# A hybrid decoder step on one core: a sixth weight buffer in one pool, and the operand sets' differences from held rows and from parts summed on GpSimd

## The chip, the cores and the metric

One core of one Trainium2 chip runs the whole kernel. Its engines work side by side, each through its own instructions in order: TensorE (PE, with its weight loads as PEld) multiplies, VectorE (DVE) and ScalarE (ACT) do elementwise work, GpSimd (Pool) does elementwise work beside them, and SyncE (SP) only issues transfers. Transfers between device memory and on-chip memory are issued from the queues of SP, ACT and Pool. The metric is the device time of one execution in microseconds; lower is better.

## The reference, cut to what matters

The reference is one step of a decoder layer for 512 prompt tokens and 64 sample tokens (8 sequences of 8), 576 columns in all, with 2048 features. What counts here are its dense products:

```
u = rmsnorm(x) @ w_in                 # 2048 x 18496: z, x/B/C, dt, q, k, v, gate, mix_s, mix_a
y = ssd(...)                          # 4096 wide, gated and group-normed
o = attention(...) * silu(g_attn)     # 2048 wide
p_ssm  = y @ w_ssm_branch             # 4096 x 2048
p_attn = o @ w_attn_branch            # 2048 x 2048
merged = sigmoid(mix_s) * p_ssm + sigmoid(mix_a) * p_attn
x = x + merged @ w_out                # 2048 x 2048
y_out = rmsnorm(x)
```

All values are fp32. Every operand is split into a rounded high part (fp32r) and a low part, and each product is made of three matmuls: high by high, high by low, low by high.

## The kernel before

Activations lie transposed: feature tiles of 128 rows by 576 columns, as pairs `hk[k]` (high `ah`, low `al`) for k = 0 to 15. A half `j` is 288 of the 576 columns (`TH`). `hb[i][j]` is the quarter of rows 8i to 8i+7 and columns of half j. The weights come in blocks of 1024 x 128 (512 KB), `raw`, and are split into `wh` (ACT, line 80) and `wl` (DVE, line 81).

Two forms of product alternate. In the plain form (`run_main`, matmuls on line 345) one output column of 128 features takes two weight blocks and 2 x 8 x 3 x 2 matmuls of 128 x 288. In the paired form (`pairs_of`, matmuls on line 453) two output columns at a time are made by a seven-product scheme of Strassen's kind: 7 x 8 x 3 matmuls instead of 8 x 8 x 3. For it the weights of a pair, A11, A21, A12 and A22, are loaded (line 380) and combined into S1 to S4 on DVE (`sum_`, line 393). The activations are combined into three further operand sets, the forms: with u1, u2 the two halves of row tile k and v1, v2 those of row tile k + 8,

```
t1 = u2 - u1        t2 = v2 - t1        t3 = v2 - u2        t6 = v1 - t2
```

t2, t3 and t6 live in the tiles `tt` (named t1k, t3k, t6k in the profile); t1 takes the place of the quarter `hb[0][1]` (called `b12`), so it is parked in device memory and brought back when the quarter is free. In a pair, product i = 2 is the first that reads it. `evict` adds up the products (line 404), `merge_out` multiplies by the gate `sg` (line 1345) and writes or accumulates into `mg_d` from Pool's queue (lines 1350 and 1352).

Stages, in order: norm and transposes; six plain columns of mix_a, beside which `sums_job` makes the first forms out of the quarters; 22 pairs for the gates and z (the first paired stage, about 123 to 628 us), beside which `bias_job` writes sixteen blocks of `bias_d` from Pool (line 491); attention; the SSD; two plain columns; then three sets: attention branch, first half of the SSM branch, second half. Each set has a **head** of four plain columns (`FIRST_OUT`) and a **run** of six pairs. Last comes w_out in the plain form.

A set begins with its activations: `acts_in` loads sixteen row tiles of 288 KB (`stg`, line 1309, SP's queue) and splits them (ACT line 1169, DVE line 1170). For the next set this is called during the last pair: rows 0 to 3 after product 2, 4 to 7 after product 3, 8 to 15 after product 6. In the head `forms_job` loads the same rows a second time (lines 1320 to 1322: u1, u2, and the whole v tile), makes t1 and t2 on DVE (1323, 1325), parks t1 from Pool's queue (1324), makes t3 and t6 on Pool (1328, 1329) and splits them all. Near the head's end the run's first weights are loaded and t1 is fetched back into eight `e` tiles.

The pools: `rs` has five tiles of 4 KB a partition, shared by the row tiles, the forms' tiles, A12, A22 and the sums; `raw` in `wp` has two, for A11, A21 and every weight block of the plain form; `ev` (tag `e`) has fourteen of 288 columns, for evictions, gates and fetched t1. A load into a tile waits until its last reader is done. The order of instructions on each engine is set by a scheduler that replays the program with its own model of times; each queue then keeps that order.

Of the kernel before, what the change touches and what calls it, by code (L numbers as in the profile page):

```python
# [34 lines left out]
OFF_XBC = DI  # L35
OFF_DT = OFF_XBC + CONV
# [19 lines left out]
N_E = 14  # L56
# [29 lines left out]
def hybrid(ctx, tc, x_prompt, x_sample, cache_k, cache_v, state_conv, state_ssm, norm_w, w_in, conv_w,  # L86
# [37 lines left out]
    mg_d = scratch([D, T], "mg_d")  # L124
    oh_d = scratch([HEADS * BL], "oh_d")
# [240 lines left out]
    def pairs_of(w, r0, cols, ops, takes, after):  # L366
# [8 lines left out]
        def load(p, *names):  # L375
            for x in names if p < n else ():
                c, kh = cols[p] + P * (x in ("A21", "A22")), x in ("A12", "A22")
                t_ = (rs if kh else wp).tile([P, 8, P], F32, tag="rs" if kh else "raw", name="raw",
                                             bufs=5 if kh else 2)
                sync.dma_start(out=t_, in_=w[r0 + 1024 * kh:r0 + 1024 * kh + 1024, c:c + P].rearrange("(k p) n -> p k n", p=P))  # L380
                st[p][x] = t_

        def sum_(p, x):
            if p >= n:
                return
            s_ = st[p]
# [6 lines left out]
            vec.tensor_tensor(out=s_[x], in0=s_[a], in1=s_[b], op=op)  # L393
# [36 lines left out]
        def run():  # L430
            for p in range(n):
                for i in range(7):
# [729 lines left out]
    b12, t1 = hb[0][1], []  # L1162
# [10 lines left out]
    def sums_job():  # L1173

        yield from wait(36)
        for k in range(8):
# [9 lines left out]
            t1.append(x[0, 0])  # L1186
# [12 lines left out]
    def t1_there():  # L1199

        for k in range(8):
            split_half(b12[k], t1[k])

    def b12_again(p, i):
        if (p, i) == (-len(cols), 0):
            t1_there()
# [12 lines left out]
    drain()  # L1219
    ms.close()  # L1220
# [57 lines left out]
    for g in range(G):  # L1278
        seq.append(m_in(OFF_XBC + (32 + g) * P, take_conv(32 + g)))
        seq.append(m_in(OFF_XBC + (40 + g) * P, take_conv(40 + g)))  # L1280
        for t in range(4):
            seq.append(m_in(OFF_XBC + (4 * g + t) * P, take_conv(4 * g + t) if t < 3 else last_x(g)))
# [20 lines left out]
    def staged_rows():  # L1303
        return rs.tile([P, 8, P], F32, tag="rs", name="stg", bufs=5).rearrange("p a b -> p (a b)")

    def acts_in(src, ks):
        for k in ks:
            t_ = staged_rows()
            sync.dma_start(out=t_[:, :T], in_=src[k * P:(k + 1) * P, :])
            split_half(hk[k], t_[:, :T])  # L1310

    tt = [[tpair(f"t{i}{k}") for k in range(8)] for i in (1, 3, 6)]

    def forms_job(src):

        for k in range(8):
            u, v = staged_rows(), staged_rows()
            u1, t1_, u2, v1, v2, t2_ = (t_[:, i * TH:(i + 1) * TH] for t_, i in ((u, 0), (u, 1), (u, 2), (v, 0), (v, 1),
                                                                            (v, 2)))
# [3 lines left out]
            vec.tensor_tensor(out=t1_, in0=u2, in1=u1, op=ALU.subtract)  # L1323
            pool.dma_start(out=xb_d[k * P:(k + 1) * P, :], in_=t1_)
            vec.tensor_tensor(out=t2_, in0=v2, in1=t1_, op=ALU.subtract)
            yield
            split_half(tt[0][k], t2_)
            pool.tensor_tensor(out=u2, in0=v2, in1=u2, op=ALU.subtract)
            pool.tensor_tensor(out=v1, in0=v1, in1=t2_, op=ALU.subtract)
            yield  # L1330
            split_half(tt[1][k], u2)
# [48 lines left out]
    for i in range(3):  # L1380
# [4 lines left out]
        def last_chunk():  # L1385
            head()
            for k in range(8):
                t1.append(etile("x"))
                sync.dma_start(out=t1[k], in_=xb_d[k * P:(k + 1) * P, :])
# [4 lines left out]
        quick.append(forms_job(src))  # L1394
# [155 lines left out]
```

## Time and profile before

| | us |
|---|---|
| runs shown: median of three (lowest to highest) | 3226.87 (3225.44 to 3229.58) |
| the profiled execution, whole | 3228.93 |
| the profiled execution, span from first to last instruction | 3226.8 |
| plain columns at the start, 24.7 to 122.6 | 97.9 |
| first paired stage, 122.7 to 628.5 | 505.8 |
| heads of the three sets | 56.2, 62.4, 61.5 |
| runs of the three sets | 135.3, 138.7, 140.1 |
| mean granted TensorE clock | 0.983 |

A page of the profile gives the busy time of each engine, the transfers and the costliest groups of instructions; L345 in it is line 345 of the kernel before. A stretch is a window of time in which the busy times are summed again. The waits of an engine name the instruction that waited and the last thing it waited for. A busy TensorE is pipelined, so the number of matmuls in a stretch says more of its pace than its busy time.

### The profile page before, as it was taken

How to read it: one execution, taken by the hardware profiler on the slowest of the kernel's cores; microseconds unless marked ns; L12 is line 12 of the kernel's file. 1: busy time of each engine (PE TensorE's matmuls, PEld its weight loads, DVE VectorE, ACT ScalarE, POOL GpSimd, SP SyncE). 2: the span in 40 equal slices, each digit the busy share in tenths (PEclk: the TensorE clock that was granted, in tenths of full speed). 3: DMA queues.
4: the chain of work that ended last, by engine and by line, in shares of the span. 5: the costliest groups of instructions: out<-in, count | busy, mean ns of one | idle time of the engine just before them, and what ended most of it. 6: DMA issues, size and time to landing. Idle time of an engine off the chain costs nothing. (4 is left out here: it accounts for less than half of the span.)

```text
span 3226.8 us, 58215 instructions
## 1 busy us (share of the span) xinstructions
PE 3112.4 (96%) x22939; PEld 2993.4 (93%) x22939; DVE 1996.5 (62%) x3434; ACT 1473.7 (46%) x2761; POOL 482.5 (15%) x591
## 2 busy tenths in 40 slices
PE   6989999999999999999999999999999999999997
PEld 5989999999898998999999999998899989998997
DVE  6656666515444443477687687686657777877354
ACT  5434444423554554455555555565433433434333
POOL 3200000000001010112213212212221031311111
PEclk9999999999999999999999999999999999999999
DMA  6564444433343243364464564565575676967655
GB/s 198 143 156 121 122 123 125 117 89 90 84 121 93 82 123 100 100 165 135 135 179 128 147 166 132 148 166 146 147 234 175 194 212 143 249 159 194 180 161 158
DMA packets 733650, 471.18 MB, mean 146 GB/s; under 512 B 45433, under 2 KB 696969, under 8 KB 733185
## 3 DMA queue, kind: packets, MB, share of 16 engines
q1 hardware_dynamic: 691616, 420.51, 46.6%
q0 software_dynamic: 24336, 29.20, 4.4%
q10 hardware_dynamic: 17424, 17.76, 1.7%
q8 instruction: 180, 2.95, 0.4%
q14 instruction: 94, 0.76, 0.1%
HBM read 385.79 MB, written 91.81 MB: 148 GB/s over the span
## 5 line engine op out<-in xcount | busy, mean ns | idle before, releaser
L80 ACT ACTIVATE wh<-raw 128x1024 fp32r<-128x1024 f32 x586 | 620.1, 1058 | 1031.6 <-PE ps L453 488.4
L81 DVE TENSOR_TENSOR wl<-raw,wh 128x1024 fp32r<-128x1024 f32 x586 | 728.0, 1243 | 529.9 <-ACT wh L80 525.9
L345 PE MATMUL ps<-ah,wh 128*128 128x288 f32 (+2 forms) x4384 | 1021.4, 302 | 34.8 <-ACT craw L828 10.1
L345 PE MATMUL ps<-ah,wl 128*128 128x288 f32 (+2 forms) x4384 | 1012.6, 301 | 3.5 <-DVE wl L81 3.3
L345 PE MATMUL ps<-al,wh 128*128 128x288 f32 (+2 forms) x4384 | 1012.4, 300 | 2.5 <-DVE al L1170 2.5
L345 PEld LDWEIGHTS ps<-ah,wh 128*128 128x128 f32 x4384 | 735.2, 192 | 50.5 <-issue 11.1
L345 PEld LDWEIGHTS ps<-ah,wl 128*128 128x128 f32 x4384 | 734.5, 191 | 19.6 <-issue 10.6
L345 PEld LDWEIGHTS ps<-al,wh 128*128 128x128 f32 x4384 | 734.6, 191 | 9.0 <-DVE al L1170 4.1
L453 PE MATMUL ps<-ah,wh 128*128 128x288 f32 x1280 | 382.2, 299 | 13.8 <-DVE w L404 5.6
L453 PE MATMUL ps<-ah,wl 128*128 128x288 f32 x1280 | 383.5, 300 | 5.9 <-DVE wl L81 5.4
L453 PE MATMUL ps<-al,wh 128*128 128x288 f32 x1280 | 381.8, 298 | 0.0
L453 PEld LDWEIGHTS ps<-ah,wh 128*128 128x128 f32 x1280 | 244.4, 191 | 14.7 <-issue 5.8
L393 DVE TENSOR_TENSOR raw<-raw 128x1024 f32<-128x1024 f32 x160 | 194.8, 1220 | 97.6 <-DMA raw<-in_w_in_dram 40.6
L453 PEld LDWEIGHTS ps<-ah,wl 128*128 128x128 f32 x1280 | 244.6, 191 | 9.3 <-DVE wl L81 9.2
L453 PEld LDWEIGHTS ps<-al,wh 128*128 128x128 f32 x1280 | 244.7, 191 | 0.1
L844 DVE SCALAR_TENSOR_TENSOR cacc<-craw,prm,cacc 128x600 f32<-128x600 f32 x144 | 126.8, 885 | 45.4 <-ACT cacc L842 43.7
L882 ACT ACTIVATE L<-L,nacs_n 128x128 f32<-128x128 f32 (+1 forms) x320 | 96.7, 379 | 56.6 <-DVE L L879 56.1
L610 DVE CUSTOM_DVE_ANT_0 sc<-bank,bm 128x256 f32<-128x256 f32 (+1 forms) x128 | 43.8, 388 | 80.0 <-PE bank L606 72.1
L923 POOL TENSOR_TENSOR xl<-xe,xh 128x512 fp32r<-128x512 f32 x32 | 58.6, 1832 | 200.3 <-ACT xh L922 199.9
L879 DVE TENSOR_TENSOR L<-L,nacs_n 128x512 f32<-128x512 f32 (+1 forms) x80 | 51.9, 662 | 47.7 <-DMA L<-nacs_d 47.3
L1093 DVE SCALAR_TENSOR_TENSOR s<-s,dec_s,bank 128x128 f32<-128x128 f32 x256 | 70.4, 340 | 10.3 <-PE bank L1087 9.3
L1241 POOL DMA_DIRECT2D dska<-in_d_skip_dram x1 | 0.6, 586 | 455.9 <-DMA z_d<-c 455.9
(575 smaller groups left out, 4497.7 us busy)
## 6 DMA issues: line engine op xcount, KB each, us to landing
raw<-in_w_in_dram SPq DMA_DIRECT2D x306, 512.0 KB
raw<-in_w_ssm_branch_dram SPq DMA_DIRECT2D x64, 512.0 KB
raw<-in_w_out_dram SPq DMA_DIRECT2D x64, 512.0 KB
L<-nacs_d SPq DMA_DIRECT2D x64, 256.0 KB
s<-in_state_ssm_dram SPq DMA_DIRECT2D x64, 256.0 KB
out_dram<-s SPq DMA_DIRECT2D x64, 256.0 KB
raw<-in_w_attn_branch_dram SPq DMA_DIRECT2D x32, 512.0 KB
stg<-y_d SPq DMA_DIRECT2D x48, 288.0 KB
```

Source lines behind the costliest of these rows:

```text
L80: pin(nc.scalar.activation(wh, raw, AF.Copy))
L81: pin(nc.vector.tensor_tensor(out=wl, in0=raw, in1=wh, op=ALU.subtract))
L345: ten.matmul(sums[i][:, s, :part.shape[1]], a[:, kk, :], part, start=(k == 0 and q == 0), stop=(k == last and q == 2))
L393: vec.tensor_tensor(out=s_[x], in0=s_[a], in1=s_[b], op=op)
L453: ten.matmul(st[p]["ps", i][:, :TH], a[:, k, :], b, start=i < 4 and k == 0 and q == 0, stop=k == 7 and q == 2, skip_group_check=i >= 4)
L610: vec.tensor_tensor_reduce(out=s_[:, i, lo:256], in0=ps[:, i, lo:256], in1=bm[j][:, i, lo:256], scale=1.0, scalar=-3e38, op0=ALU.add, op1= ...
L844: vec.scalar_tensor_tensor(out=acc[:, :600], in0=raw[:, i:i + 600], scalar=prm[:, i * 48 + j:i * 48 + j + 1], in1=acc[:, :600], op0=ALU.mu ...
L879: vec.tensor_tensor(out=l_[:rows, :, :n], in0=l_[:rows, :, :n], in1=nacs_n[:rows, blk, h:h + 4].unsqueeze(2).to_broadcast([rows, 4, n]), o ...
L882: act.activation(l_[:rows, i, :n], l_[:rows, i, :n], AF.Exp, scale=-1.0, bias=nacs_n[:rows, blk, h + i:h + i + 1])
L923: pool.tensor_tensor(out=xl, in0=xe, in1=xh, op=ALU.subtract)
L1093: vec.scalar_tensor_tensor(out=sts[i][:, t, :], in0=sts[i][:, t, :], scalar=dec_s[:, 4 * g + t, b:b + 1], in1=ps[:, v, i, :], op0=ALU.mult ...
L1241: pool.dma_start(out=dska, in_=AP(d_skip, 0, [[0, P], [1, H]]))
```

## The change

What the change does:

- The `rs` pool has six tiles instead of five, `ev` eleven instead of fourteen. A21 is loaded into an `rs` tile, so that only A11 is left of a pair in `raw`; the next pair's loads are asked for in the order A21, A22, A11.
- In the first stage t1 goes to a new buffer in device memory, `t1_d`, and is fetched back after the six plain columns; before, it stayed in eight `e` tiles.
- In `acts_in` the sixteen row loads move from SP's queue to Pool's. The tiles of rows 8 to 11 are kept (`staged`, `N_HELD`).
- In `forms_job` u1 and u2 are no longer loaded: one Pool add of high and low part makes both. For k = 0 to 3 v is the kept tile; for k = 4 to 7 it is loaded as before. t3 and t6 are made on DVE instead of Pool.

The renamed offset in the diff (`OFF_XBC`) changes nothing else.

```diff
-N_E = 14
+N_HELD = 4
+N_E = 11
...
+    t1_d = scratch([D // 2, TH], "t1_d")
...
-                t_ = (rs if kh else wp).tile([P, 8, P], F32, tag="rs" if kh else "raw", name="raw",
-                                             bufs=5 if kh else 2)
+                t_ = weights_tile() if x != "A11" else wp.tile([P, 8, P], F32, tag="raw", name="raw", bufs=2)
...
-                s_[x] = rs.tile([P, 8, P], F32, tag="rs", name="raw", bufs=5)
+                s_[x] = weights_tile()
...
-                        load(p + 1, "A11", "A21", "A22")
+                        load(p + 1, "A21", "A22", "A11")
...
+    def weights_tile(name="raw"):
+        return rs.tile([P, 8, P], F32, tag="rs", name=name)
...
-                       for n_, b_ in (("tx", 1), ("rs", 5), ("ev", N_E))))
+                       for n_, b_ in (("tx", 1), ("rs", 6), ("ev", N_E))))
...
-            t1.append(x[0, 0])
+            pool.dma_start(out=t1_d[k * P:(k + 1) * P, :], in_=x[0, 0])
...
     drain()
+    for k in range(8):
+        t1.append(etile("x"))
+        sync.dma_start(out=t1[k], in_=t1_d[k * P:(k + 1) * P, :])
     ms.close()
...
     def acts_in(src, ks):
         for k in ks:
             t_ = staged_rows()
-            sync.dma_start(out=t_[:, :T], in_=src[k * P:(k + 1) * P, :])
+            pool.dma_start(out=t_[:, :T], in_=src[k * P:(k + 1) * P, :])
             split_half(hk[k], t_[:, :T])
+            if 8 <= k < 8 + N_HELD:
+                staged.append(t_)
...
-    def forms_job(src):
+    def forms_job(src, rows):
         for k in range(8):
-            u, v = staged_rows(), staged_rows()
...
-            sync.dma_start(out=u1, in_=src[k * P:(k + 1) * P, :TH])
-            sync.dma_start(out=u2, in_=src[k * P:(k + 1) * P, TH:])
-            sync.dma_start(out=v[:, :T], in_=src[1024 + k * P:1024 + (k + 1) * P, :])
+            u = staged_rows()
+            u1, t1_, u2 = (u[:, i * TH:(i + 1) * TH] for i in range(3))
+            pool.tensor_tensor(out=u[:, :3 * TH].rearrange("p (a b) -> p a b", a=3)[:, 0:3:2, :], in0=sq(hk[k][0]),
+                               in1=sq(hk[k][1]), op=ALU.add)
+            if k < len(rows):
+                v = rows[k]
+            else:
+                v = staged_rows()
+                sync.dma_start(out=v[:, :T], in_=src[1024 + k * P:1024 + (k + 1) * P, :])
+            v1, v2, t2_ = (v[:, i * TH:(i + 1) * TH] for i in range(3))
+            yield
             vec.tensor_tensor(out=t1_, in0=u2, in1=u1, op=ALU.subtract)
-            pool.dma_start(out=xb_d[k * P:(k + 1) * P, :], in_=t1_)
+            pool.dma_start(out=t1_d[k * P:(k + 1) * P, :], in_=t1_)
             vec.tensor_tensor(out=t2_, in0=v2, in1=t1_, op=ALU.subtract)
+            vec.tensor_tensor(out=u2, in0=v2, in1=u2, op=ALU.subtract)
             yield
             split_half(tt[0][k], t2_)
-            pool.tensor_tensor(out=u2, in0=v2, in1=u2, op=ALU.subtract)
-            pool.tensor_tensor(out=v1, in0=v1, in1=t2_, op=ALU.subtract)
+            split_half(tt[1][k], u2)
+            vec.tensor_tensor(out=v1, in0=v1, in1=t2_, op=ALU.subtract)
             yield
-            split_half(tt[1][k], u2)
             split_half(tt[2][k], v1)
             yield
```

The scheduler places the instructions anew. Three places matter for what follows; a row is a line of the kernel (before or after), the operation, what it writes and reads, the shape of a tile, and how often it repeats.

Pool's queue between the first and the second set, before: the last pair's writes of w, o and the two c, then the forms of the second set.

```order
L1352 DMA mg_d<-w 128x288
L1352 DMA mg_d<-o 128x288
L1352 DMA mg_d<-c 128x288 x2
L1324 DMA xb_d<-stg 128x288
L1328 TENSOR_TENSOR stg<-stg 128x288
```

The same place after, with the row loads (line 1315) and the adds (1329):

```order
L1315 DMA stg<-y_d 128x576 x7
L1367 DMA mg_d<-w 128x288
L1315 DMA stg<-y_d 128x576 x3
L1367 DMA mg_d<-o 128x288
L1315 DMA stg<-y_d 128x576 x2
L1367 DMA mg_d<-c 128x288 x2
L1315 DMA stg<-y_d 128x576 x2
L1329 TENSOR_TENSOR stg<-ah_227,al_228 128x2x288
L1329 TENSOR_TENSOR stg<-ah_229,al_230 128x2x288
L1339 DMA t_d<-stg 128x288 x2
```

The row loads have come in among the writes; the last two of them, rows 14 and 15, stand behind both c. Next SP's queue at the end of the second head, before: `raw` on line 73 is the plain form's weight block, on line 380 the first pair's; x is t1 on its way back.

```order
L1320 DMA stg<-y_d 128x288
L1321 DMA stg<-y_d 128x288
L1341 DMA sg<-ms_d 128x288
L1322 DMA stg<-y_d 128x576
L380 DMA raw<-in_w_ssm_branch_dram 128x8x128 x2
L1341 DMA sg<-ms_d 128x288
L380 DMA raw<-in_w_ssm_branch_dram 128x8x128 x2
L1341 DMA sg<-ms_d 128x288
L380 DMA raw<-in_w_ssm_branch_dram 128x8x128
L1389 DMA x<-xb_d 128x288 x8
```

And after:

```order
L1335 DMA stg<-y_d 128x576 x2
L1356 DMA sg<-ms_d 128x288
L382 DMA raw<-in_w_ssm_branch_dram 128x8x128
L1335 DMA stg<-y_d 128x576
L382 DMA raw<-in_w_ssm_branch_dram 128x8x128 x4
L1356 DMA sg<-ms_d 128x288
L1404 DMA x<-t_d 128x288 x8
```

Of the forms' loads only four of 288 KB are left on SP (the last three stand here), and the first pair's weights follow them directly. Last Pool's queue in the first plain columns, before, where `out_dram<-in_cache` are copies of the caches:

```order
L1181 DMA xb_d<-x 128x288
L1251 DMA sinks_s<-sink_d 64x4x1 x2
L529 DMA out_dram<-in_cache_k_dram 2x4x15360 x4
L529 DMA out_dram<-in_cache_v_dram 2x4x15360 x4
L1181 DMA xb_d<-x 128x288 x7
```

And after:

```order
L1186 DMA xb_d<-x 128x288
L1191 DMA t_d<-x 128x288
L1186 DMA xb_d<-x 128x288
L1191 DMA t_d<-x 128x288
L1186 DMA xb_d<-x 128x288 x2
L1191 DMA t_d<-x 128x288 x2
```

The writes of t1 alternate with those of the quarter, and the cache copies are gone from here: they now follow the sixteen bias writes and the load of `dska`.

More of the change, by code (lines that the diff above doesn't have):

```diff
@@ L34 @@
 NEG = -1e30
-OFF_XBC = DI
-OFF_DT = OFF_XBC + CONV
+OFF_xb_dC = DI
+OFF_DT = OFF_xb_dC + CONV
 OFF_Q = OFF_DT + H
@@ L1197, in hybrid @@
     back = []
-    def t1_there():
-        for k in range(8):
-            split_half(b12[k], t1[k])
+    t1 = []
     def b12_again(p, i):
         if (p, i) == (-len(cols), 0):
-            t1_there()
+            for k in range(8):
+                split_half(b12[k], t1[k])
         elif (p, i) == (-1, 1):
@@ L1219, in hybrid @@
     drain()
+    for k in range(8):
+        t1.append(etile("x"))
+        sync.dma_start(out=t1[k], in_=t1_d[k * P:(k + 1) * P, :])
     ms.close()
@@ L1278, in hybrid @@
     for g in range(G):
-        seq.append(m_in(OFF_XBC + (32 + g) * P, take_conv(32 + g)))
-        seq.append(m_in(OFF_XBC + (40 + g) * P, take_conv(40 + g)))
+        seq.append(m_in(OFF_xb_dC + (32 + g) * P, take_conv(32 + g)))
+        seq.append(m_in(OFF_xb_dC + (40 + g) * P, take_conv(40 + g)))
         for t in range(4):
-            seq.append(m_in(OFF_XBC + (4 * g + t) * P, take_conv(4 * g + t) if t < 3 else last_x(g)))
+            seq.append(m_in(OFF_xb_dC + (4 * g + t) * P, take_conv(4 * g + t) if t < 3 else last_x(g)))
         seq += left[:MIXES_S[g]]
@@ L1303, in staged_rows @@
     def staged_rows():
-        return rs.tile([P, 8, P], F32, tag="rs", name="stg", bufs=5).rearrange("p a b -> p (a b)")
+        return weights_tile("stg").rearrange("p a b -> p (a b)")
     def acts_in(src, ks):
@@ L1388, in last_chunk @@
                 t1.append(etile("x"))
-                sync.dma_start(out=t1[k], in_=xb_d[k * P:(k + 1) * P, :])
+                sync.dma_start(out=t1[k], in_=t1_d[k * P:(k + 1) * P, :])
         head, run = pairs_of(w, r0, [n * P for n in range(FIRST_OUT, KT, 2)], ops,
@@ L1393, in hybrid @@
                              on_products((KT - FIRST_OUT) // 2, t1, nxt, sets[i + 1][2], *sets[i + 1][:2], 14 if i == 2 else KT))
-        quick.append(forms_job(src))
+        quick.append(forms_job(src, staged[-N_HELD:]))
         run_main([(w_loads(w, r0, n * P), hx, by_halves(takes[n])) for n in range(FIRST_OUT)], raws=raws, then=last_chunk)
```

5 lines of the change are left out of this document (2 added, 3 removed).

## The prediction

> **What bounds the kernel now.** I read the page first, then a table of stretches, then what each engine waits for in the worst stretches. The page's first rows:
>
> ```profile
> span 3226.8 us, 58215 instructions
> PE 3112.4 (96%) x22939; PEld 2993.4 (93%) x22939; DVE 1996.5 (62%) x3434; ACT 1473.7 (46%) x2761; POOL 482.5 (15%) x591
> ```
>
> TensorE is the bound, so a change can only win where TensorE stands still. The table of stretches shows where that is; its columns are the stretch, its length, then busy time and instruction count of each engine, granted clock, DMA share and GB/s:
>
> ```profile
> 300.00:400.00 100.00, 100.00 (x758) 100.00 (x757) 68.96 (x74) 40.36 (x53) 0.00 (x0) 1.00 0.43 121
> 24.70:122.60 97.90, 91.06 (x643) 86.93 (x641) 76.40 (x172) 47.28 (x104) 19.97 (x27) 0.98 0.51 148
> 122.70:628.50 505.80, 496.31 (x3702) 494.37 (x3701) 331.54 (x357) 205.17 (x274) 18.55 (x19) 0.99 0.49 130
> 2377.90:2434.10 56.20, 51.64 (x386) 51.21 (x384) 44.23 (x65) 21.96 (x43) 22.80 (x29) 1.00 0.89 276
> 2434.10:2569.40 135.30, 135.23 (x1008) 135.17 (x1009) 101.85 (x131) 52.61 (x61) 13.49 (x25) 0.99 0.54 159
> 2569.40:2631.80 62.40, 55.09 (x386) 53.98 (x384) 46.25 (x70) 25.69 (x47) 24.61 (x31) 0.95 0.93 273
> 2631.80:2770.50 138.70, 137.33 (x1008) 135.50 (x1009) 100.18 (x131) 51.00 (x59) 21.28 (x25) 0.99 0.66 152
> 2770.50:2832.00 61.50, 53.83 (x386) 52.71 (x384) 48.77 (x71) 25.54 (x46) 26.05 (x31) 0.97 0.98 278
> 2832.00:2972.10 140.10, 137.44 (x1008) 136.53 (x1009) 101.86 (x133) 51.91 (x61) 19.55 (x23) 0.98 0.65 154
> 2972.10:3005.10 33.00, 24.75 (x122) 22.05 (x121) 15.50 (x29) 10.84 (x17) 0.00 (x0) 0.80 0.96 300
> ```
>
> The first row is undisturbed: 758 matmuls in 100 us, 0.132 us each. At that pace the 384 matmuls of a head (the four unpaired columns of a set) need 50.7 us and the 1008 of a run (its six pairs) 133.0. So the heads lose 56.2 - 50.7 = 5.5, 11.7 and 10.8 us, the runs 2.3, 5.7 and 7.1. The first paired stage (122.7 to 628.5) loses 505.8 - 3702 x 0.1319 = 17.4 us, and the stretch after the last run 33.0 - 16.1 = 16.9. In the heads DMA stands at 0.89 to 0.98, DVE at only 44 to 49 us. The transfers and DVE's waits of the second head (line, what it waited for, us in total, times, longest):
>
> ```profile
> DMA packets 19384, 17.03 MB, mean 273 GB/s; under 512 B 1177, under 2 KB 17293, under 8 KB 19379
> stg<-y_d SPq DMA_DIRECT2D x12, 288.0 KB
> stg<-y_d SPq DMA_DIRECT2D x16, 144.0 KB
> ```
>
> ```profile
> DVE raw L393 <- DMA raw<-in_w_ssm_branch_dram: 5.6, 1, 5.6
> DVE al L1170 <- ACT ah L1169: 3.8, 2, 2.1
> DVE stg L1325 <- DMA stg<-y_d: 3.5, 3, 1.6
> DVE stg L1323 <- DMA stg<-y_d: 2.7, 3, 1.4
> ```
>
> 11.8 of the 15.6 us are waits for loads. How that reaches TensorE, from DVE's and then TensorE's row of time (start, length, instruction, idle time before it):
>
> ```profile
> 2615.36 0.45 DVE L1170 TENSOR_TENSOR t36l<-stg,t36h 128x288 fp32r<-128x288 f32 x1
> 2615.73 0.45 DVE L1345 TENSOR_TENSOR o<-ps,sg 128x288 f32<-128x288 f32 x1
> 2616.10 1.03 DVE L1325 TENSOR_TENSOR stg<-stg 128x288 f32<-128x288 f32 x1
> 2626.32 1.23 DVE L393 TENSOR_TENSOR raw<-raw 128x1024 f32<-128x1024 f32 x1 [5.63 <-DMA raw<-in_w_ssm_branch_dram]
> 2627.47 0.45 DVE L1345 TENSOR_TENSOR o<-ps,sg 128x288 f32<-128x288 f32 x1
> 2631.24 0.45 DVE L1345 TENSOR_TENSOR o<-ps,sg 128x288 f32<-128x288 f32 x1
> ```
>
> ```profile
> 2631.84 0.37 PE L453 MATMUL ps<-ah,wh 128*128 128x288 f32 x1 [2.49 <-ACT wh L80]
> ```
>
> The first weight sum of the run (L393) waits 5.63 us for its load; the evictions of a finished column (L1345) queue behind it; TensorE starts the run only after them.
>
> **The change, term by term, against the profiled execution's own 3228.9 us.**
>
> *Heads, memory.* A set's forms now load 8 x (2 x 144 + 288) KB = 4.72 MB. Four rows of 288 KB (1.18 MB) stay, so 3.54 MB of the second head's 17.03 go: 13.5 MB, 49.4 us at 273 GB/s, just under TensorE's 50.7. Memory stops being the bound; what is late next is DVE.
>
> *Heads, DVE.* Sixteen subtractions come over from Pool. Neighbours in DVE's row start 0.37 us apart (2615.36, 2615.73), so +5.9 us. Pool's two-input work goes from 16 short operations to 8 longer ones:
>
> ```profile
> L1329 POOL TENSOR_TENSOR stg<-stg 128x288 f32<-128x288 f32 x8 | 8.5, 1059 | 2.1 <-issue 2.1
> L1328 POOL TENSOR_TENSOR stg<-stg 128x288 f32<-128x288 f32 x8 | 7.6, 945 | 3.5 <-DMA stg<-y_d 3.4
> L976 POOL TENSOR_TENSOR sqr<-xc 128x576 f32<-128x576 f32 x24 | 33.5, 1395 | 1.3
> ```
>
> No row shows an add of two rounded parts; the nearest is L976, of the same 576 elements, 1.40 us, so 8 x 1.4 = 11.2 us for 16.1. DVE is slowed while Pool works (1.03 us instead of 0.45 at 2616.10); that falls by between 0 and 4.9 us, I take 2. DVE's busy time becomes 48, 50 and 53 us. Its waits were 62.4 - 46.3 = 16 us in the second head; without the form loads for four rows and with free memory I leave 5: the weight sum still waits for slots (five of the six `rs` tiles belong to a pair now, and they come free only as the forms end), and four rows are still loaded. Heads of about 54, 55 and 58 us: -2, -7, -4, together **-13**. Bounds: 50.7 us each (-28), and DVE's 5.9 us with all waits kept (+18).
>
> *Heads, what is moved past Pool's queue.* The sixteen row loads go to Pool, and there rows 14 and 15 stand behind both writes of the last pair's c. Four held rows also leave two tiles for rows 12 to 15. In the second head the rows were:
>
> ```profile
> 2579.24 0.54 POOL L1352 DMA_DIRECT2D mg_d<-c  x1 [3.52 <-DMA raw<-in_w_ssm_branch_dram]
> 2581.67 0.76 DVE L1170 TENSOR_TENSOR al<-stg,ah 128x576 fp32r<-128x576 f32 x1 [2.06 <-ACT ah L1169]
> mg_d<-o POOLq DMA_DIRECT2D x5, 144.0 KB, 4.4
> ```
>
> If that write stayed at 2579.24, row 15 would be issued at about 2581, land up to 4.4 us later and be split 1.4 us after that: 2587 where DVE did it at 2581.67. But DVE was there late because row loads were late; at its own pace c's write comes some 4 us earlier. I take +1 for the two transitions, bounds 0 and +10. SP in turn loses sixteen loads a set, each of which waited for a tile.
>
> *Runs.* With sums less late, part of the slow clock after each start goes; A21 no longer waits for the single `raw` ring: **-3** (bounds -8, 0). Eleven `e` tiles instead of fourteen hold back gate loads: in a run a pair takes ten, so each is reused one pair later, **+1** (0 to +15, what the runs lose now).
>
> *First columns.* The eight cache copies leave their place ahead of `xb_d`:
>
> ```profile
> out_dram<-in_cache_k_dram POOLq DMA_DIRECT2D x4, 480.0 KB, 13.9
> 55.10 0.59 POOL L1181 DMA_DIRECT2D xb_d<-x  x1 [9.87 <-DMA out_dram<-in_cache_k_dram]
> 61.91 0.95 DVE L1184 TENSOR_TENSOR x<-x 128x288 f32<-128x288 f32 x2 [5.48 <-DMA xb_d<-x]
> ```
>
> ```profile
> POOL dska L1241 <- DMA z_d<-c: 455.9, 1, 455.9
> ```
>
> DVE's 5.48 us go; TensorE, which waits after it, gains less: **-3** (-6 to +3: sixteen more transfers, and t1 must return by the third product). The copies now stand behind Pool's transfer of `dska`, which the last row shows waiting 455.9 us (until about 645), in a stage where loads have room: **+1** (0 to +10).
>
> *First paired stage.* The sixteen bias writes remain; they hold memory and the sums' loads:
>
> ```profile
> bias_d<-oh_d POOLq DMA_DIRECT2D x16, 383.0 KB, 22.0
> 192.99 1.23 DVE L393 TENSOR_TENSOR raw<-raw 128x1024 f32<-128x1024 f32 x1 [11.13 <-DMA raw<-in_w_in_dram]
> ```
>
> A21 and A22 are now asked for a product (3.2 us = 24 x 0.132) or so earlier, and the sixth tile lets them: **-4** (-10 to +4). *After the last run* the chain that ended last goes through w_out's loads, behind the residual's:
>
> ```profile
> 2985.04 13.26 DMA raw<-in_w_out_dram
> ```
>
> Both stay; only the row loads leave SP: **-1** (-6 to +4). In all -13 + 1 - 3 + 1 - 3 + 1 - 4 - 1 = **-21**, 3208 us; the median of the runs shown is 2.1 us under the profiled one, so 3206.
>
> A rule bears on the Pool adds. The Trainium skill (SBUF — State Buffer, "SBUF: two separate sides") says that a DVE operation with two SBUF inputs and a Pool operation that reads SBUF share a port pair by an exclusive lock, the later one waiting for the other's whole instruction. The row at 2616.10 agrees in kind (1.03 for 0.45 us beside Pool). By it each add could shut DVE out for its full 1.4 us, which speaks against the change; it is weighed in the last rival.
>
> **Rivals.** (1) *Late rows.* DVE reaches the last c as late as now, rows 14 and 15 stall TensorE by about 5 us twice, clock loss included: 3206 + 10 = 3216. For it: both writes stand ahead in Pool's order and only two tiles circulate; against it: what made DVE late goes. (2) *Hidden anyway.* Tiles, not memory, set when A21 and A22 come: S1 still waits its 5 us, the forms' saving ends in the same wait, the extra 5.9 us on DVE eat the rest; -4 from the start and flood alone, 3223. For it: SP's loads wait for DVE; against it: DMA at 0.93. (3) *Slower: Pool's add becomes the gate.* Row k+2's add needs the tile that DVE frees with row k, so DVE and Pool take turns (7 x 0.37 + 1.4 us and a handover each), now in place of the loads' waits. Then DVE keeps its 16 us of waits and has 5.9 more work: +5.9 in three heads, +18, nothing won in the runs or in the flood, -3 at the start: 3242. It decides once DVE's waits in a head stay above 16 - 5.9, about 10 us. That last rival is the one which the skill's lock makes likelier. (4) *More relief.* Heads at TensorE's pace and half of the flood: 3226.9 - 28 - 8 - 8 = 3183.
>
> **How the numbers follow.** Within 0.2% (6.5 us) is about what a measurement cannot tell from no change: 3220 to 3233. Forecast, 3206: 0.50, with an own range of 3194 to 3217; late rows 0.17 (about a third of it within 0.2%); hidden 0.12; slower 0.13; more relief 0.08. Faster 0.50 + 0.08 + 0.10 = 0.68; same 0.18; slower 0.14. The range takes all of the first three, a part of the others: 3184 to 3234.
>
> **What would show it.** Right: DMA in the heads clearly under 0.9 with some 13.5 MB; no wait of 5 us before the first weight sum; heads of 54 to 58 us with DVE above 48. Late rows: TensorE idle at the second half of a head's first column, behind al. Pool as gate: DVE waits for Pool's line of adds, heads over 62 us. Wrong altogether if the DMA share falls and the heads stay at 62, or if the time moves elsewhere: in the SSD stage, which no term here touches, or at 645 us.

## The result, and the profile after

The change makes the kernel slower: 3257.59 us, median of four runs (3254.26 to 3259.93), beside 3228.22 (3225.44 to 3231.49) for the kernel before; the ratio is 1.0097, with a 95% interval of 1.0081 to 1.0112. The forecast was 3206, within 3184 to 3234: wrong in sign and outside the range.

The page's first rows, after:

```profile
span 3252.5 us, 58133 instructions
PE 3116.8 (96%) x22939; PEld 2997.7 (92%) x22939; DVE 2014.9 (62%) x3482; ACT 1475.3 (45%) x2763; POOL 516.0 (16%) x637
```

TensorE does the same 22939 matmuls. Its busy time grows by 4.4 us and the span by 25.7, so most of the loss is time in which it stands still. The table of stretches of the kernel after shows where (columns as before: stretch, length, then busy time and count of PE, PEld, DVE, ACT and POOL, granted clock, DMA share, GB/s). The rows are the first columns, the first paired stage, then head and run of each of the three sets, and the stretch after the last run:

```profile
22.70:118.40 95.70, 90.35 (x643) 86.58 (x642) 73.34 (x164) 44.46 (x98) 16.05 (x19) 0.98 0.50 141
118.40:632.50 514.10, 497.60 (x3703) 495.96 (x3702) 334.81 (x365) 205.96 (x282) 20.55 (x23) 0.98 0.49 128
2385.90:2439.70 53.80, 51.28 (x385) 51.04 (x384) 44.03 (x77) 20.70 (x39) 23.89 (x23) 1.00 0.68 204
2439.70:2579.90 140.20, 136.64 (x1008) 135.45 (x1009) 105.36 (x136) 55.91 (x68) 20.95 (x39) 0.99 0.54 161
2579.90:2641.10 61.20, 53.16 (x387) 52.73 (x385) 47.91 (x82) 20.89 (x38) 26.95 (x25) 0.96 0.72 198
2641.10:2787.80 146.70, 139.43 (x1008) 138.05 (x1009) 105.01 (x134) 55.17 (x66) 28.93 (x39) 0.97 0.62 152
2787.80:2850.50 62.70, 53.24 (x386) 52.56 (x385) 48.81 (x84) 21.61 (x39) 27.92 (x26) 0.96 0.75 199
2850.50:3000.30 149.80, 140.49 (x1009) 139.13 (x1010) 106.03 (x137) 56.47 (x69) 27.33 (x37) 0.96 0.61 150
3000.30:3033.30 33.00, 25.19 (x131) 22.38 (x131) 14.65 (x27) 9.63 (x14) 0.03 (x1) 0.84 0.94 289
```

DMA in the second and third head has fallen from 0.93 and 0.98 to 0.72 and 0.75, as forecast; the heads have hardly become shorter. The runs are 4.9, 8.1 and 9.6 us longer. To set kernels side by side, each stage is measured from its first matmul to the next stage's first, by the count of matmuls; one profiled execution each, us. A stage ends with the next stage's first matmul, so a wait of TensorE just ahead of that matmul counts with the stage that ends:

| | first columns | first paired | between | heads, sum | runs, sum | after the runs |
|---|---|---|---|---|---|---|
| before | 98.0 | 505.9 | 1749.4 | 180.2 | 414.0 | 242.3 |
| after | 95.7 | 514.1 | 1753.4 | 177.7 | 436.7 | 239.8 |

The first matmul starts at 22.7 us instead of 24.7, so -2.0; the stages give -2.3, +8.2, +4.0, -2.5, +22.7 and -2.5. That makes +25.6, the 25.7 of the two spans within rounding.

**The runs.** The second run, before: first one of DVE's waits, then one of TensorE's (line, what it waited for, us in total, times, longest):

```profile
DVE raw L393 <- issue: 12.8, 4, 3.7
```

```profile
PE ps L453 <- DVE wl L81: 0.9, 2, 0.7
```

The same in the second run after (L393 is L395 now, L81 is L83, L453 is L455):

```profile
DVE raw L395 <- issue: 15.5, 4, 4.0
```

```profile
PE ps L455 <- DVE wl L83: 7.2, 5, 2.4
```

"issue" stands where the profile shows nothing that ended the wait; the weight loads on SP's queue show below what DVE waited for. DVE's wait at a weight sum is old: 12.8 us then, 15.5 now. That TensorE then waits for a low weight part is new: 0.9 us then, 7.2 now. The pages show the same for the whole kernel, before and then after (busy and mean, then the waits):

```profile
L453 PE MATMUL ps<-ah,wl 128*128 128x288 f32 x1280 | 383.5, 300 | 5.9 <-DVE wl L81 5.4
```

```profile
L455 PE MATMUL ps<-ah,wl 128*128 128x288 f32 x1280 | 386.6, 302 | 33.4 <-DVE wl L83 33.4
```

Of these 33.4 us, 16.5 lie in the first paired stage and 16.9 in the three runs (1.0, 7.2 and 8.7), where it was 3.5 before. So the low part makes some 13 of the runs' 22.7 us. By the starts of the matmuls some 3 us are other waits, and some 6.5 are matmuls that start further apart than 0.132 us. What changed is what stands behind the sum. DVE's row of time in a pair of the second run, before (start, length, instruction, idle time before it):

```profile
2687.22 0.45 DVE L404 TENSOR_TENSOR u<-ps,p 128x288 f32<-128x288 f32 x1
2687.59 1.21 DVE L81 TENSOR_TENSOR wl<-raw,wh 128x1024 fp32r<-128x1024 f32 x1
2691.92 1.23 DVE L393 TENSOR_TENSOR raw<-raw 128x1024 f32<-128x1024 f32 x1 [3.12 <-issue]
2693.06 0.45 DVE L404 TENSOR_TENSOR w<-ps,u 128x288 f32<-128x288 f32 x1
```

And the same place in the kernel after:

```profile
2704.69 1.22 DVE L395 TENSOR_TENSOR raw<-raw 128x1024 f32<-128x1024 f32 x1 [3.98 <-issue]
2705.84 0.45 DVE L406 TENSOR_TENSOR u<-ps,p 128x288 f32<-128x288 f32 x1
2706.20 1.22 DVE L395 TENSOR_TENSOR raw<-raw 128x1024 f32<-128x1024 f32 x1
2707.34 1.22 DVE L83 TENSOR_TENSOR wl<-raw,wh 128x1024 fp32r<-128x1024 f32 x1
```

TensorE began product 4 at 2706.26 and stood still for its low part:

```profile
2708.61 0.40 PE L455 MATMUL ps<-ah,wl 128*128 128x288 f32 x1 [1.92 <-DVE wl L83]
```

The sum is S1 of the next pair (L393, now L395); the low part next to it is that of product 4, which TensorE needs soon. Before, u and this low part came first and DVE then waited 3.12 us for S1's weights with nothing urgent behind it. After, S1 comes first, waits 3.98 us, and u, a second sum and the low part queue behind it. In each of the five pairs of this run that have a successor, TensorE waits at just this place of product 4, for 0.4 to 2.4 us. SP's row puts the last weight load ahead of it 5.4 us earlier:

```profile
2699.24 0.38 SPq L382 DMA_DIRECT2D raw<-in_w_ssm_branch_dram  x1
```

**The heads.** DVE's waits in the second head after, then TensorE's at its start:

```profile
DVE al L1175 <- ACT ah L1174: 3.9, 1, 3.9
DVE wl L83 <- ACT wh L82: 3.6, 1, 3.6
DVE stg L1338 <- POOL stg L1329: 2.3, 2, 1.3
DVE raw L395 <- DMA raw<-in_w_ssm_branch_dram: 2.1, 1, 2.1
DVE o L1360 <- DMA sg<-ms_d: 1.4, 1, 1.4
```

```profile
PE ps L348 <- ACT ah L1174: 3.8, 1, 3.8
```

The waits for form loads are gone and the first weight sum waits 2.1 us instead of 5.6, as forecast. But 13.3 us of waits are left where 5 were forecast, and TensorE waits 3.8 us for the high part of a row tile. At the head's end it waits once more, until an eviction (`o`, L1360) is done:

```profile
2641.05 0.58 PE L455 MATMUL ps<-ah,wh 128*128 128x288 f32 x1 [4.20 <-DVE o L1360]
```

These two waits are 8.0 of the 10.5 us that the head takes beyond TensorE's own pace. And this is what the eight adds on Pool (L1329) take in that head (busy us, mean ns):

```profile
L1329 POOL TENSOR_TENSOR stg<-ah,al 128x576 f32<-128x576 f32 x8 | 16.6, 2089 | 8.8 <-DVE al L1175 5.0 <-DVE t32l L1175 3.7
```

2.09 us each, not the 1.40 of the estimate: 16.6 us, more than the 16.1 of the subtractions they replace. In the rows of time, first DVE's, then Pool's, adds and single DVE instructions lengthen each other:

```profile
2619.46 2.63 DVE L83 TENSOR_TENSOR wl<-raw,wh 128x1024 fp32r<-128x1024 f32 x1
2623.85 2.28 DVE L1341 TENSOR_TENSOR stg<-stg 128x288 f32<-128x288 f32 x1
```

```profile
2615.26 3.79 POOL L1329 TENSOR_TENSOR stg<-ah,al 128x576 f32<-128x576 f32 x1 [3.67 <-DVE t32l L1175]
2619.55 1.44 POOL L1329 TENSOR_TENSOR stg<-ah,al 128x576 f32<-128x576 f32 x1
2624.08 1.72 POOL L1329 TENSOR_TENSOR stg<-ah,al 128x576 f32<-128x576 f32 x1
```

The low part at 2619.46 takes 2.63 instead of 1.21 us, 1.42 more, beside an add of 1.44; the subtraction at 2623.85 takes 2.28 instead of 0.45, 1.83 more, beside an add of 1.72. That is not new, though. Add up, over the second head, what DVE's instructions took beyond the median of their shape, where that was more than 0.1 us: it comes to some 8.8 us in the kernel before, beside sixteen subtractions on Pool, and some 8.4 us after, beside eight adds.

### The profile page after: what moved, and what is told of

The parts are those of the page before. It is cut to its first block, busy times and chain, and to the rows that moved or that the text cites. A ratio compares the mean times of both kernels' runs of the same rounds, so it can differ in the third digit from the quotient of the medians.

```text
span 3252.5 us, 58133 instructions
## 1 busy us (share of the span) xinstructions
PE 3116.8 (96%) x22939; PEld 2997.7 (92%) x22939; DVE 2014.9 (62%) x3482; ACT 1475.3 (45%) x2763; POOL 516.0 (16%) x637
## 5 line engine op out<-in xcount | busy, mean ns | idle before, releaser
L83 DVE TENSOR_TENSOR wl<-raw,wh 128x1024 fp32r<-128x1024 f32 x586 | 735.9, 1256 | 564.9 <-ACT wh L82 562.3
L455 PE MATMUL ps<-ah,wl 128*128 128x288 f32 x1280 | 386.6, 302 | 33.4 <-DVE wl L83 33.4
L455 PE MATMUL ps<-ah,wh 128*128 128x288 f32 x1280 | 385.2, 301 | 14.5 <-DVE o L1360 14.5
L455 PE MATMUL ps<-al,wh 128*128 128x288 f32 x1280 | 384.4, 300 | 0.0
L455 PEld LDWEIGHTS ps<-ah,wl 128*128 128x128 f32 x1280 | 247.4, 193 | 37.2 <-DVE wl L83 37.1
L395 DVE TENSOR_TENSOR raw<-raw 128x1024 f32<-128x1024 f32 x160 | 195.2, 1222 | 112.3 <-DMA raw<-in_w_in_dram 48.1
L455 PEld LDWEIGHTS ps<-ah,wh 128*128 128x128 f32 x1280 | 247.6, 193 | 15.8 <-issue 15.8
L455 PEld LDWEIGHTS ps<-al,wh 128*128 128x128 f32 x1280 | 247.5, 193 | 0.6 <-issue 0.5
```

The source lines that it names most:

```text
L83: pin(nc.vector.tensor_tensor(out=wl, in0=raw, in1=wh, op=ALU.subtract))
L455: ten.matmul(st[p]["ps", i][:, :TH], a[:, k, :], b, start=i < 4 and k == 0 and q == 0, stop=k == 7 and q == 2, skip_group_check=i >= 4)
```

## The experiments

Three theories stood at the start. **Q**: the place of S1 in DVE's queue costs the runs their 22 us. **E**: the missing `e` tiles hold gate loads back. **F**: the forms' part (row loads from Pool, adds on Pool, more subtractions on DVE). Ratios are to the kernel before on the same chip, with the 95% interval. The stage sums are of one profiled execution each, which lies up to 7.2 us from its kernel's median (f1: 3235.82 beside 3228.63), so a difference of a few us in a stage can be scatter. Three chips were used; the kernel before takes 3224.60 us on that of e2, e3, e5 and e7, 3220.12 on that of e4, e8, e9 and e10, and 3220.45 on that of the f runs. The ranges are in microseconds, so a hit or a miss by less than 4.5 us says little in e4, e8, e9 and e10; the ratios are not touched by this.

| | ratio | first paired | heads, sum | runs, sum |
|---|---|---|---|---|
| before | 1 | 505.9 | 180.2 | 414.0 |
| after | 1.0097 (1.0081 to 1.0112) | 514.1 | 177.7 | 436.7 |
| e2, 14 `e` tiles | 1.0101 (1.0086 to 1.0116) | 513.9 | 179.4 | 434.3 |
| e3, before with 11 `e` tiles | 0.9994 (0.9981 to 1.0007) | 505.0 | 179.5 | 411.8 |
| e5, A21 in `raw` again | 1.0019 (1.0010 to 1.0029) | 511.3 | 175.8 | 420.5 |
| e7, S1 behind product 4 | 1.0012 (1.0003 to 1.0022) | 509.2 | 175.8 | 413.0 |
| e4, weights part alone | 1.0051 (1.0035 to 1.0067) | 513.0 | 168.8 | 428.4 |
| e8, e7 and row loads on SP | 0.9997 (0.9988 to 1.0006) | 507.5 | 176.4 | 408.0 |
| e9, e7 and adds on DVE | 0.9965 (0.9954 to 0.9977) | 507.2 | 161.9 | 413.4 |
| e10, e7 and gate loads on ACT | 1.0013 (1.0002 to 1.0024) | 507.6 | 173.1 | 414.5 |
| f1, after with adds on DVE | 1.0021 (1.0012 to 1.0031) | 513.8 | 167.1 | 424.2 |
| f2, e9 and row loads on SP | 0.9937 (0.9923 to 0.9952) | 507.3 | 155.8 | 408.3 |
| f3, e9 and idle adds on Pool | 1.0028 (1.0018 to 1.0037) | 507.2 | 168.2 | 425.0 |
| f4, e4 with S1 behind product 4 | 0.9970 (0.9960 to 0.9981) | 506.9 | 169.0 | 406.3 |

**The `e` tiles.** Fourteen in the kernel after:

```diff
-N_E = 11
+N_E = 14
```

> The kernel after, with fourteen e tiles instead of eleven (both stages that use the pool); nothing else. Theory Q (DVE's queue): in each run the first weight sum S1 of the next pair now stands ahead of the low part wl of product 4, and waits there some 4 us for its load; e tiles do not matter: 3252 to 3260, the yearly pair gaps of 1.2 to 2.5 us behind wl stay. Theory E (e tiles): gate loads are held back by the missing three tiles, and the runs' loss goes: 3234 to 3242. Theory F (forms and row loads): as after, 3252 to 3260.

3258.08 us ("yearly" in the text above is a slip for "repeated"). And eleven in the kernel before, in the stage of the three sets:

```diff
-    def pair_pools():
+    def pair_pools(n_e=N_E):
...
-                       for n_, b_ in (("tx", 1), ("rs", 5), ("ev", N_E))))
+                       for n_, b_ in (("tx", 1), ("rs", 5), ("ev", n_e))))
...
-    stk, tx, rs, ev = pair_pools()
+    stk, tx, rs, ev = pair_pools(11)
```

> The kernel before, with eleven e tiles in the stage of the three sets only (fourteen stay in the first paired stage); nothing else. Theory Q: as before, 3224 to 3233, since the order on every engine is the one of before. Theory E: the runs lose what they lose in the kernel after, 3242 to 3250. Theory F: as before.

3223.18 us beside 3224.60. Putting the tiles back changes nothing and taking them away changes nothing: theory E is out.

**Where A21 lies, and where S1 stands.** First A21 and the load order as before, all else as after:

```diff
-                t_ = weights_tile() if x != "A11" else wp.tile([P, 8, P], F32, tag="raw", name="raw", bufs=2)
+                t_ = weights_tile() if kh else wp.tile([P, 8, P], F32, tag="raw", name="raw", bufs=2)
...
-                        load(p + 1, "A21", "A22", "A11")
+                        load(p + 1, "A11", "A21", "A22")
```

> The kernel after, but A21 is loaded into the raw ring again, in the order A11, A21, A22, as before; six rs tiles, eleven e tiles, the held rows, Pool's adds, row loads from Pool and t1_d stay. In the runs DVE's queue then again has u and the wl of product 4 ahead of S1. Theory Q: the runs (+22 us together) and the first paired stage (+8) come back, so 3222 to 3232; no repeated gaps behind wl. Theory E: the runs stay as in the kernel after, 3248 to 3258. Theory F: 3248 to 3258 too.

3230.80 us, in Q's range. The runs come back from 436.7 to 420.5, not all the way. Then one statement alone is moved:

```diff
                     elif i == 3:
-                        sum_(p + 1, "S1")
                         load(p + 1, "A12")
                     elif i == 4:
+                        sum_(p + 1, "S1")
                         sum_(p + 1, "S2")
```

> The kernel after, with one statement moved: in a run S1 of the next pair is asked for behind product 4 instead of product 3 (load rules, tiles and forms all as in the kernel after). The order of DVE's queue in a run is then that of before (u and the wl of product 4 ahead of S1). Theory Q: the runs' gaps behind wl go, 3226 to 3238. Theory E: runs stay, 3250 to 3260. Theory F: 3250 to 3260.

3227.49 us, in Q's range: of the 0.97% this one statement gives back 0.85, some 27 us. Runs 413.0. DVE's and TensorE's waits in its second run:

```profile
DVE raw L395 <- issue: 8.6, 3, 3.2
```

```profile
PE ps L455 <- DVE wl L83: 0.7, 2, 0.4
```

TensorE's waits for the low part fall from 7.2 to 0.7 us. With the statement moved, the scheduler also puts SP's weight and gate loads in pairs again, as before the change. The two were not tried apart, but the gaps that went are the ones behind the low part, and DVE's waits for gates in this run did not get shorter (`c` behind `sg`: 12.6 us in the kernel after, 18.2 in e7).

**The weights part alone**: forms, adds and row loads as before the change, the rest as after.

```diff
-            pool.dma_start(out=t_[:, :T], in_=src[k * P:(k + 1) * P, :])
+            sync.dma_start(out=t_[:, :T], in_=src[k * P:(k + 1) * P, :])
...
-        quick.append(forms_job(src, staged[-N_HELD:]))
+        quick.append(forms_job(src))
```

(with `forms_job` as it was before the change, t1 parked in `t1_d`)

> The weights part of the change alone: six rs tiles, A21 in an rs tile, load order A21, A22, A11, eleven e tiles, t1_d in the first stage; the row loads stay on SP and the forms are loaded twice and subtracted on Pool as before. DVE's queue in the runs is that of the kernel after (S1 ahead of u and the wl of product 4). Theory Q (this order is the loss): the runs lose about 22 us together and the first paired stage some 8, heads as before: 3244 to 3258. Rival (the loss needs row loads or adds on Pool as well): 3222 to 3234.

3239.47 us: below Q's range (by the other chip's 3224.60 it would be 3241), above the rival's. The runs do lose without any part of the forms, 14.4 us of the 22.7, and the first paired stage 7.1. What Q did not foresee: the heads fall to 168.8, 11.4 us under those of before. So the weights part (the sixth tile, A21 in it and the order of the loads, which were not tried apart) relieves the heads by itself, and the forms' part as written takes that back (177.7). With S1 moved as well, the same edit as in e7:

> The weights part alone (e4: forms loaded twice, Pool's subtractions, row loads on SP as before), with S1 behind product 4. Theory Q: its runs fall from 428.4 to about 412 us together and the first paired stage by 4, its heads stay near 169: 3214 to 3224. If the forms' part is worth nothing, it stands level with e9: 3205 to 3212.

3211.74 us, a little below the first range: runs 406.3, heads 169.0, and faster than before by 0.30%.

**What the forms' part costs.** Three edits on e7, one each. The row loads from SP's queue:

```diff
-            pool.dma_start(out=t_[:, :T], in_=src[k * P:(k + 1) * P, :])
+            sync.dma_start(out=t_[:, :T], in_=src[k * P:(k + 1) * P, :])
```

> The kernel with S1 behind product 4 (e7), and the row loads back on SP's queue instead of Pool's. Theory L (rows 14 and 15 are late because they stand behind both c writes on Pool): TensorE's wait of 1.8 to 4.5 us in a head's first column, behind the high part of a late row, goes, heads two and three come from 59.0 and 62.7 to 55 to 59, in all 3217 to 3224. Rival T (two free rs tiles hold rows 12 to 15 back whichever queue loads them): the wait stays, 3225 to 3232.

3220.78 us, in theory L's range, but not for the reason given: the heads stay (176.4). The runs show 5 us less, but this profiled execution is 4.9 us faster than the median of its kernel, so that may be scatter. In the second head TensorE's wait for the row's high part is gone, and another stands in its place:

```profile
PE ps L348 <- DVE o L1360: 4.6, 1, 4.6
```

The adds on DVE:

```diff
-            pool.tensor_tensor(out=u[:, :3 * TH].rearrange("p (a b) -> p a b", a=3)[:, 0:3:2, :], in0=sq(hk[k][0]),
+            vec.tensor_tensor(out=u[:, :3 * TH].rearrange("p (a b) -> p a b", a=3)[:, 0:3:2, :], in0=sq(hk[k][0]),
```

> The kernel with S1 behind product 4 (e7), and the eight adds of high and low part made on DVE instead of Pool. Theory P (an add on Pool holds DVE up: beside adds of 1.4 to 3.8 us single DVE instructions take 2.3 instead of 0.44 us): DVE gains about as much as eight more instructions cost it, its waits for the adds (2.3 us a head) go, heads 2 to 4 us shorter each: 3217 to 3225. Rival D (DVE is the bound of a head now, and eight more instructions of 0.7 us or more lengthen it): heads 2 to 6 us longer each, 3231 to 3242.

3208.62 us beside 3220.12, better than theory P's range: the heads fall by 13.9 us to 161.9, where 2 to 4 us each were expected. The adds in its second head, now in DVE's list, and the head's stretch (2568.3 to 2622.2):

```profile
L1329 DVE TENSOR_TENSOR stg<-ah,al 128x576 f32<-128x576 f32 x8 | 5.8, 758 | 0.0
```

```profile
2568.30:2622.20 53.90, 51.40 (x386) 51.17 (x385) 45.57 (x96) 21.57 (x43) 11.88 (x18) 1.00 0.82 226
```

DVE makes the eight adds as well, and is busy for 45.57 us in this head; in e7 it was 47.05, in the kernel after 47.91. No DVE instruction in this head runs 0.1 us over the median of its shape any more. And the gate loads of a head from ACT's queue:

```diff
-            sync.dma_start(out=sg, in_=gate_d[rows, cs])
+            (act if n < FIRST_OUT else sync).dma_start(out=sg, in_=gate_d[rows, cs])
```

> The kernel with S1 behind product 4 (e7), and the gate loads of the four plain columns of each set on ACT's queue instead of SP's. Theory G (at a head's end TensorE waits 4.5 us for an eviction, which waits for a gate load that SP issued behind the weight loads): the wait falls to 2 or 3 us, 3218 to 3225. Rival: the weight sums' own loads set it, or ACT is held up by its loads: 3225 to 3235.

3222.11 us lies in theory G's range, but only because this chip is the faster one: the ratio is 1.0013 beside e7's 1.0012, so nothing is won. The wait itself did fall, from 4.6 to 3.4 us ahead of the second run and from 4.5 to 2.0 ahead of the third. So theory G had the wait right, at least in part, and its worth wrong.

**Two losses, or one?** The kernel after with the adds on DVE and nothing else:

> The kernel after with one edit: the eight adds of a set on DVE instead of Pool; S1 stays ahead in DVE's queue. Theory A (two separate losses, the adds in the heads and the order in the runs): heads of about 162 us together instead of 177.7, runs as in the kernel after (434 to 437), 3238 to 3248. Rival: the heads' gain needs the other order as well, 3250 to 3259.

3228.63 us, some 9 us under theory A's range. The heads come to 167.1, but the runs gain too, 436.7 to 424.2. The two losses overlap: with S1 moved (27 us) or the adds moved (24 us) either edit alone brings back most of the 0.97%; both together give 1.32%, some 42 us, less than the sum of the two. TensorE's waits for the low part are still 28.9 us in f1, beside 33.4 after. What moving S1 is worth in the runs thus depends on the rest: 23.7 us in the kernel after, 22.1 in e4 (428.4 to 406.3), 10.8 in f1 (424.2 to 413.4 in e9). Why the runs of f1 gain with S1 still in front was not resolved.

**Is it the adding itself?** In e9, beside each add on DVE, the same add on Pool into a tile that nothing reads:

```diff
+    junk = tx.tile([P, 2, TH], F32, tag="junk", name="junk")
...
+            pool.tensor_tensor(out=junk, in0=sq(hk[k][0]), in1=sq(hk[k][1]), op=ALU.add)
```

> S1 behind product 4, adds on DVE (e9), and beside each of them an add of the same shape and the same operands on Pool into a tile that nothing reads. Theory P (it is Pool's adding itself that holds DVE up, whoever needs the sum): heads back to 170 to 177 us together, single DVE instructions of 2 us and more beside Pool's adds, 3217 to 3226. Rival (it was DVE's waiting for the sums, a matter of who depends on whom): heads 160 to 165, 3205 to 3213.

3227.97 us: 24 adds that nobody needs take back the whole gain of e9 (0.9965 to 1.0028), which is more than theory P expected. The time is not all where it was expected either: heads 168.2, a little under theory P's range, and the runs 425.0, where the second one starts with a wait for weights:

```profile
PE ps L455 <- ACT wh L82: 4.6, 1, 4.6
```

In its second head DVE's list shows a part of it (mean ns of the low weight parts and of the rows' low parts), and Pool's the idle adds:

```profile
L83 DVE TENSOR_TENSOR wl<-raw,wh 128x1024 fp32r<-128x1024 f32 x8 | 11.3, 1417 | 0.0
L1175 DVE TENSOR_TENSOR al<-stg,ah 128x576 fp32r<-128x576 f32 x9 | 7.8, 885 | 5.0 <-ACT ah L1174 5.0
```

```profile
L1333 POOL TENSOR_TENSOR junk<-ah,al 128x576 f32<-128x576 f32 x5 | 7.6, 1528 | 0.1
```

1417 and 885 ns stand beside 1226 and 756 in e9: 8 x 0.19 + 9 x 0.13 = 2.7 us in this head. How these become some 6 us a set in heads and runs is not resolved. Pool's writes of t1 also stand behind the idle adds, so f3 shows that work on Pool which nobody waits for costs this time, but not that all of it comes through longer DVE instructions.

**The row loads again, with DVE on time**: e9 with e8's edit.

> S1 behind product 4, adds on DVE (e9), and the row loads back on SP. Theory L (with DVE on time the rows' place behind both c writes on Pool is what is left, 2.7 and 4.4 us in heads two and three): heads 152 to 158 us together instead of 161.9, 3198 to 3206. Rival T (the wait only changes its name, as it did with the row loads on SP and the adds on Pool, where an eviction was 4.7 and 6.2 us late in its place): 3206 to 3214.

3201.12 us beside 3220.45, ratio 0.9937 (0.9923 to 0.9952): faster than both kernels, and by 0.63% faster than the one before. Its page, and the second head and run:

```profile
span 3201.3 us, 58131 instructions
PE 3098.3 (97%) x22939; PEld 2982.2 (93%) x22939; DVE 2007.3 (63%) x3506; ACT 1474.0 (46%) x2763; POOL 434.6 (14%) x551
```

```profile
2568.50:2620.50 52.00, 51.31 (x386) 51.10 (x385) 45.77 (x90) 19.96 (x37) 9.85 (x15) 1.00 0.83 223
2620.50:2758.00 137.50, 134.44 (x1009) 133.77 (x1010) 104.86 (x135) 55.75 (x68) 21.30 (x25) 1.00 0.67 165
```

The head takes 52.0 us, 1.3 over TensorE's own pace, and TensorE's only listed wait in it is this, at its end:

```profile
PE ps L455 <- DVE o L1360: 0.7, 1, 0.7
```

Here theory L holds: once DVE is on time, the rows' place in Pool's queue is worth 6 us in the heads and 5 in the runs (e9 to f2).

## Why the prediction was wrong, by its own steps

**Runs, -3: this step failed, and it is most of the error.** Measured: +22.7. The prediction priced the weights part as relief (a ring less to wait for) and looked at the SP and Pool queues for what the scheduler had moved, but not at DVE's in a run. There A21's new tile moved S1 ahead of u and product 4's low part. DVE's wait for the sum's weights grew little (12.8 to 15.5 us in the second run); an old wait, which had held nothing up, came to stand in front of something that TensorE needs each pair. e7 shows it: one statement, 27 us, of which 23.7 in the runs. The first run is the exception: it is 4.9 us longer with only 1.0 us of waits for the low part.

**First paired stage, -4:** measured +8.2, the same code. With S1 moved it is at +3.3 (e7), +1.4 (f2) and +1.0 (f4). Seven kernels run this stage with S1 moved (e7 to e10, f2 to f4); they lie between 506.9 and 509.2, so 1 to 3 us of loss remain, and the relief of 4 us that the prediction expected shows in none.

**Heads, -13: measured -2.5.** The memory step held: DMA share 0.72 and 0.75, 198 GB/s x 61.2 us = 12.1 MB in the second head against 13.5 forecast. The step on DVE's waits failed: 5 us were left to it, 13.3 are there. Its premise on Pool was the wrong size: 8 x 1.4 = 11.2 us of adds were 16.6. What DVE loses beside Pool was to fall "by between 0 and 4.9 us, I take 2"; it fell from some 8.8 to some 8.4. DVE's busy time was still below the forecast (47.91 for 50), so it is the waits that failed. With the adds on DVE the heads give -18.3, with the row loads on SP too -24.4, near the bound of -28: the relief was there, and larger than forecast, but the adds used it up. Part of it (11.4 us, e4) comes from the weights part, which the prediction did not count in the heads.

**Late rows, +1:** TensorE does wait behind them, 3.8 us in the second head. The wait cost little while DVE was late anyway (e8: only its name changed) and 9 us in all once it was not (0.9965 to 0.9937). The prediction argued that at DVE's own pace the last write of c comes some 4 us earlier, and rows 14 and 15 with it. It was issued 9.8 us after the second head's start before, 9.1 us after, and still 7.3 in e9, where DVE is on time; there TensorE waits 2.5 and 4.2 us for the high part of a row in the second and third head. So the argument did not hold.

**`e` tiles, +1 (0 to +15):** zero, from both sides (e2, e3).

**First columns -3, caches +1, after the last run -1:** -2.3 (and 2.0 before the first matmul), +4.0 for all that lies between, -2.5. One execution each, and kernels with the same code ahead of it differ as much in the first columns (95.7 for the kernel after, 99.7 for e2); these were not tried by themselves. The prediction's place for the cache copies, 645 us, is also a misreading: the transfer of `dska` ahead of them is issued at 633.3.

**The rivals.** The third came nearest, 3242 for 3257.59 measured. Its test was that DVE's waits in a head stay above 10 us: 13.3. Its mechanism, Pool and DVE taking turns, is there, though DVE waits only 2.3 us for sums; the turns lengthen instructions instead. But its price, +18 us in the heads, is not: the heads did not become longer, and the runs, where it saw nothing, did. The prediction's last sentence named the true case, that the DMA share falls, the heads stay at 62 and "the time moves elsewhere", but not the runs as the place. The Trainium skill (SBUF — State Buffer, "Who interferes with whom") says that a DVE instruction with two SBUF inputs and a Pool instruction that reads SBUF lock each other out for a whole instruction. The trace agrees in size: +1.42 us beside an add of 1.44, +1.83 beside 1.72. Which of the two came first it does not show, as Pool's spans are rough. By that rule the prediction's 1.40 us an add was the price of an add that meets a gap (1.44 here), not of one that must wait for DVE.

## What to carry to other kernels

Where a scheduler lays out the queues, look at the order of every engine in the steady loop before pricing a change of buffers, and ask of each wait what stands behind it: a wait that was free can become the bound without growing. Work moved to an idle engine is not free if the two engines lengthen each other's instructions; here eight adds cost 5.8 us on DVE and 16.6 on Pool, and DVE was the busier for not having them. When a relief does not show, take the added pieces out one by one: here the place of one sum and that of eight adds hid a gain of 0.35% (e9), and the row loads another 0.28% (f2).

## What the runs showed of the hardware

A Pool add seems to be held up through several DVE instructions, not one. The add that started at 2615.26 took 3.79 us. DVE's row in that time begins and ends like this:

```profile
2615.47 0.45 DVE L1338 TENSOR_TENSOR stg<-stg 128x288 f32<-128x288 f32 x1
...
2617.31 0.44 DVE L1341 TENSOR_TENSOR stg<-stg 128x288 f32<-128x288 f32 x1
2617.68 0.44 DVE L1360 TENSOR_TENSOR o<-ps,sg 128x288 f32<-128x288 f32 x1
2619.08 0.46 DVE L1338 TENSOR_TENSOR stg<-stg 128x288 f32<-128x288 f32 x1 [0.96 <-POOL stg L1329]
```

Six instructions with two operands in on-chip memory run 0.37 us apart from 2615.47 to 2617.31; then comes one that reads PSUM, then a gap. The add ends at 2619.05, 1.37 us after the start of the one that reads PSUM, about the time of an add left alone (1.44). So it seems to have stood still until then; Pool's spans in the profile are rough, and this was not tried by itself.

A wait of TensorE can cost more than its own length. Behind the 4.2 us wait that ends at 2641.05 in the kernel after, the next 24 matmuls start 0.24 us apart instead of 0.13 and take 5.9 us instead of 3.2. The granted clock of the second head goes with the waits: 0.95 before and 0.96 after, with 7.3 and 8.0 us of TensorE's waits; 1.00 in e9 and f2, with 2.5 and 0.7.
